# One matmul of 128 columns per level in the heads of a recurrent layer, with the second token half stored in another order

## The chip, the cores and the metric

The kernel runs on one core of a Trainium2 chip. The metric is the device time of one execution in microseconds (us), as the median of several runs.

## The reference, cut to what matters

A decoder trunk of two layers for 256 tokens of 2048 features. Layer 0 mixes tokens by two recurrences side by side, layer 1 by attention; an MLP follows each. The change concerns the second group of layer 0, eight heads (`hgrn2`) with 128 keys and 128 values each, and at its edge the first group (`rg_lru`).

```python
q = jax.nn.silu(q_raw.astype(F32))
log_f = jnp.log(lower_bound + (1.0 - lower_bound) * jax.nn.sigmoid(fz))
k = (1.0 - lower_bound) * jax.nn.sigmoid(-fz)
...
b = jnp.cumsum(gc, axis=2)
o_inter = jnp.einsum('bhtk,bhkv->bhtv', qc * jnp.exp(b), state)
decay = jnp.exp(jnp.where(causal, b[:, :, :, None, :] - b[:, :, None, :, :], -jnp.inf))
scores = jnp.einsum('bhtk,bhsk,bhtsk->bhts', qc, kc, decay)
o_intra = jnp.einsum('bhts,bhsv->bhtv', scores, vc)
```

So every query token sees every earlier key token of its head, each of the 128 key features damped by the product of the forget gates between the two tokens. The first group is a convolution over four tokens, two gates from block-diagonal products, a linear recurrence along the tokens, and a product with a GeLU branch.

## The kernel before, in words

**Matmuls.** TensorE (PE) multiplies 128x128 stationary blocks with moving columns. The inputs of the large products are split in two parts, `hi` and `lo`, and three products replace one (hi·hi, lo·hi, hi·lo). Weights come from HBM as `raw` tiles of 128x2048 by DMAs that SyncE (SP) issues. ScalarE (ACT) casts each into `hi` (L117) in two halves of 1024 columns, and VectorE (DVE) subtracts to get `lo` (L118). All three tiles have 3 buffers. The product itself is in `mm` (L205). What carries `bufa,hi` or `bufa,lo` in the profile are projections of the normed input, 48 matmuls of 256 columns (all tokens) for 128 features.

**The recurrent stage** (up to about 320 us of the span) is a list of steps in the string `ORDER` (L1172): `h0` to `h7` are the heads (`hgrn`), `x0` to `x7` the inputs of the first group (`lru_in`), `g0` and `g1` its gates (`lru_gates`, four blocks each), `y0` to `y7` its outputs (`lru_out`), `v`, `k`, `p` and `f` values, gates and prepared forms. A scheduler merges the steps' instructions when the kernel is built, with priorities that the source gives; on the chip each engine runs its list in order. So the string moves instructions on every engine.

**A head** projects q and f (two projections), then treats pairs of tokens (`pd`, L470), and then doubles: at level c = 2, 4, ..., 64 the tokens stand in blocks of 2c, and the second c queries of each block meet the first c keys. The tile `qk` holds q and k, 128 features on the partitions, 256 tokens each. A level (L483 to L514) is two f32 matmuls, one per half of 128 tokens (L492): the half's keys are the stationary block, all 128 of them, and 64 of its queries are the moving columns. The result `pl` has rows for all 128 keys, of which those in the right block are wanted. For c up to 16 a masked copy on DVE (L495) puts them into `st`; at c = 32 ACT copies two pieces of 32x64 (L500), at c = 64 one of 64x128 (L502). Then DVE scales q and k in place by the gates of the block (L509), for the next level, and makes the products of twice the length (L511). At c = 128 one matmul of 128 columns (L487) does the first half's keys against the second half's queries. `st` times the values gives `po` (L516 to L518); ACT squares it (L522), DVE norms it, and PE transposes it (L530) into `bufb`.

**lru_in** scales the projected block into `xp` (L538 and L418 in the profile), ACT applies the first tap (L540), DVE the other three (L542), and the result is split into `bufb` (ACT cast L250, DVE L251). **lru_gates** (L547) makes eight products of six matmuls from pairs of those blocks, each evicted by an ACT sigmoid (L234); tanh, exp and sqrt on ACT, products (L560) and a scan (L569) on DVE follow. **lru_out** multiplies its branch with the scan's result (L580). Projections and gate products share three PSUM banks (`p`), a level's result has two buffers (`pl`).

Of the kernel before, what the change touches and what calls it, by code (L numbers as in the profile page):

```python
# [10 lines left out]
F32 = mybir.dt.float32  # L11
# [9 lines left out]
P = 128  # L21
# [21 lines left out]
def trunk_kernel(ctx, tc, begin, xtok, cols, tab, masks, pos, fin, w_in, w_gate, w_out, w_qkv, w_o, w1, w2, out):  # L43
# [383 lines left out]
    def halves(t, c, second):  # L427
        return t.rearrange("p (n two c) -> p n two c", two=2, c=c)[:, :, int(second), :]
# [19 lines left out]
    def hgrn(hd, vg, gg):  # L448
        u0 = 20 + (hd // 4) * 16 + (hd % 4) * 2
        oml = omlb[:, hd:hd + 1]  # L450
        qk = wk.tile([P, 2 * S], F32, name="qk", bufs=3)
        qp, kq = qk[:, :S], qk[:, S:]
        p = project(w_in, u0, bufx)
        z = normed(p, "hz", 4)
        lut(qp, z, AF.Sigmoid)
        q3 = wk.tile([P, P, 3], F32, name="q3", bufs=2)
        pairs_ = lambda t: t.rearrange("p (n two) -> p n two", two=2)
        V.scalar_tensor_tensor(q3[:, :, :2], pairs_(z), oml, pairs_(qp), op0=OP.mult, op1=OP.mult)
        p = project(w_in, u0 + 1, bufx)
        z = normed(p, "hz", 4)  # L460
        f = wk.tile([P, S], F32, name="f", bufs=3)
        lut(f, z, AF.Sigmoid)
        lut(kq, z, AF.Sigmoid, scale=-1.0)
        V.tensor_scalar(f, f, oml, lb[:, hd:hd + 1], op0=OP.mult, op1=OP.add)
        f2 = pairs_(f)
        V.tensor_tensor(q3[:, :, 2], q3[:, :, 1], f2[:, :, 1], OP.mult)
        pd = psc.tile([P, P, 3], F32, name="pd", bufs=1)
        for j in range(2):
            js = slice(64 * j, 64 * j + 64)
            T.matmul(pd[:, js].rearrange("p n c -> p (n c)"), kq[:, j * P:j * P + P],  # L470
                     q3[:, js].rearrange("p n c -> p (n c)"), start=True, stop=True)
        st = wk.tile([P, 3, P], F32, name="st", bufs=3)
        V.tensor_tensor(st[:, :2].rearrange("p j (n two) -> p j n two", two=2),
                        pd[:, :, :2].rearrange("p (j n) c -> p j n c", j=2),
                        pairs_(ident)[:, None].to_broadcast([P, 2, 64, 2]), OP.mult)
        stf = st[:, :2].rearrange("p a b -> p (a b)")
        V.copy_predicated(halves(stf, 1, True), msk[:, 0].rearrange("p (n c) -> p n c", c=1), pd[:, :, 2:])
        V.tensor_tensor(pairs_(qp), q3[:, :, ::2], f2[:, :, :1].to_broadcast([P, P, 2]), OP.mult)
        V.tensor_tensor(pairs_(kq)[:, :, 0], pairs_(kq)[:, :, 0], f2[:, :, 1], OP.mult)
        tot = wk.tile([P, P], F32, name="tot128", bufs=2)  # L480
        V.tensor_tensor(tot, f2[:, :, 0], f2[:, :, 1], OP.mult)
        c = 2
        while c <= 128:  # L483
            pl = psc.tile([P, 2, 64], F32, name="pl", bufs=2)
            if c == 128:
                plf = pl.rearrange("p j c -> p (j c)")
                T.matmul(plf, kq[:, :P], qp[:, P:], start=True, stop=True)  # L487
                A.copy(st[:, 2], plf)
                break
            for j in range(2):  # L490
                js = slice(j * P, j * P + P)
                T.matmul(pl[:, j], kq[:, js], halves(qp[:, js], c, True), start=True, stop=True)  # L492
            if c <= 16:
                lv = LEVELS.index(c)
                V.copy_predicated(halves(stf, c, True), msk[:, lv].rearrange("p (n c) -> p n c", c=c),  # L495
                                  pl.rearrange("p j (n c) -> p (j n) c", c=c))
            elif c == 32:
                for n in range(2):
                    ps_ = slice(64 * n, 64 * n + 32)
                    A.copy(st[ps_, :2, 64 * n + 32:64 * n + 64], pl[ps_, :, 32 * n:32 * n + 32])  # L500
# [8 lines left out]
            V.tensor_tensor(both, both, fac, OP.mult)  # L509
# [6 lines left out]
        T.matmul(po[:, 0], st[:, 0], vg[:, 0, vs], start=True, stop=True)  # L516
        T.matmul(po[:, 1], st[:, 2], vg[:, 0, vs], start=True, stop=False)
# [15 lines left out]
    xc = wk.tile([P, 8, S], F32, name="xc", bufs=1)  # L533

    def lru_in(b):
        p = project(w_in, b, bufx)
        xp = wk.tile([P, S + 4], F32, name="xp", bufs=1)
        V.memset(xp[:, :4], 0.0)  # L538
        scaled(p, xp[:, 4:])
        A.activation(xc[:, b], xp[:, 4:], AF.Identity, bias=col("conv_b", b), scale=col("conv_w", 24 + b))  # L540
        for i in range(3):
            V.scalar_tensor_tensor(xc[:, b], xp[:, 1 + i:1 + i + S], col("conv_w", 8 * i + b), xc[:, b],  # L542
                                   op0=OP.mult, op1=OP.add)
        split_to(bufb[:, b], xc[:, b])
# [38 lines left out]
    def part_forms(f, k, m, at, src):  # L583
# [577 lines left out]
NOSYNC = mybir.DependencyInfo(mybir.DependencyClass.NoSync, mybir.DependencyReason.DATA)  # L1161


def _tables():
    ident = np.eye(P, dtype=np.float32)
    q = np.arange(S)[:, None]
    k = np.arange(S)[None, :]
    d = q - k
# [12 lines left out]
    for lv, c_ in enumerate(LEVELS):  # L1181
        col = np.arange(64)[None, :]
        m = (s // (2 * c_) == col // c_) & (s % (2 * c_) < c_)
        masks[:, lv, :64] = m
        masks[:, lv, 64:] = m
    return tab, masks


# [3 lines left out]
def _layout(a):  # L1192
# [33 lines left out]
    for what in ATTENTION:  # L1226
# [7 lines left out]
    xf = n(a["x"]).reshape(S, KB, P).transpose(2, 1, 0)  # L1234
    return {
        "begin": c(np.concatenate([xf, fv[:4].reshape(4, P, 4, 512).transpose(1, 0, 2, 3).reshape(P, KB, 512)], axis=2)),
        "xtok": c(n(a["x"]).reshape(2, P, D).transpose(1, 0, 2)),
        "cols": c(np.concatenate(cols, axis=1)),
        "tab": tab, "masks": masks,
        "pos": c(n(a["positions"]).reshape(2, P).T),  # L1240
        "fin": c(n(a["final_norm"]).reshape(1, D)),
        "w_in": c(np.concatenate(w_in)), "w_gate": c(w_gate), "w_out": c(toks(n(a["rec_w_out"][0]), [(k + 8) % KB for k in PAIRED])),
        "w_qkv": c(np.concatenate(w_qkv)), "w_o": c(toks(n(a["attn_w_o"][0]), PAIRED)),
# [20 lines left out]
```

## Time and profile before

| | |
|---|---|
| runs | 2122.53 us median of 3 (2121.95 to 2122.95) |
| profiled execution | 2123.78 us |
| its span | 2122.0 us |
| granted TensorE clock, mean | 0.999 |
| PE busy | 2111.1 us, 99% |
| DVE busy | 1807.3 us, 85% |
| ACT busy | 1383.3 us, 65% |

The profile is one execution. PE, DVE and ACT are the engines; PEld is the loading of stationary blocks, which can run beside PE's matmuls. A row of a timeline gives start, duration, engine, line of the source, operation, output and inputs, the stationary block's shape, and the moving shape. An f32 matmul leaves two records (x2), since it takes two passes. A list of waits gives for an engine's line whom it waited for, the total, how often, and the longest. A row of a group gives count, busy time, mean ns of one, and the idle time ahead of it.

### The profile page before, as it was taken

What the parts mean: (1) busy time and instruction counts of PE and PEld (TensorE: products, weight loads), DVE (VectorE), ACT (ScalarE), POOL (GpSimd) and SP (SyncE); (2) the same over time, 40 slices, a digit from 0 to 9 for tenths busy, and PEclk for the clock granted to TensorE, in tenths of its full rate; (3) what the DMA queues carried; (4) which work ended last, traced back from release to release, by engine and by line L of the source; (5) the groups of instructions that cost most, each with busy time, mean ns of one, the idle gap of its engine ahead of it and who ended that gap; (6) DMA issues with size and microseconds to landing.
All of it is one profiled execution on the core that took longest, in us unless ns stands there. A gap on an engine that the chain in (4) does not pass through costs nothing.

```text
span 2122.0 us, 26673 instructions
## 1 busy us (share of the span) xinstructions
PE 2111.1 (99%) x10492; PEld 1788.3 (84%) x10492; DVE 1807.3 (85%) x1998; ACT 1383.3 (65%) x1543; POOL 69.6 (3%) x89
## 2 busy tenths in 40 slices
PE   9999999999999999999999999999999999999998
PEld 8989998888888888888888888888888888888886
DVE  6987888888888888888987797798888887988887
ACT  7554666676576476567767777776755765755764
POOL 0000000000000000000000000000000000000000
PEclk9999999999999999999999999999999999999999
DMA  8565446877786777687887677777777768777874
GB/s 341 180 217 179 159 155 204 253 261 221 220 272 231 229 237 252 228 253 240 261 261 239 213 211 258 258 232 233 237 240 256 240 214 261 244 231 229 271 227 146
DMA packets 70382, 492.90 MB, mean 232 GB/s; under 512 B 7872, under 2 KB 8384, under 8 KB 12016
## 3 DMA queue, kind: packets, MB, share of 16 engines
q1 hardware_dynamic: 57888, 410.17, 51.6%
q0 software_dynamic: 11792, 79.89, 19.7%
q8 instruction: 82, 1.34, 0.2%
q10 hardware_dynamic: 576, 1.13, 0.1%
q14 instruction: 44, 0.36, 0.0%
HBM read 486.97 MB, written 4.19 MB: 231 GB/s over the span
## 4 chain that ended last, share of the span: by engine, by line
PE 98%; ACT 1%; DVE 1%; issue 0%; DMA 0%; SPq 0%; ACTq 0%; DVEq 0%
PE p L205 61%; PE po L205 14%; PE pd L205 13%; PE pt L205 5%; PE pl L208 2%; PE pl L492 1%; PE pl L205 0%; ACT hi L117 0%; ACT gi L234 0%; PE pd L208 0%; PE pd L470 0%; ACT L234 0%; DMA first<-in_begin 0%; ACT gr L234 0%; DVE xc L569 0%
## 5 line engine op out<-in xcount | busy, mean ns | idle before, releaser
L118 DVE TENSOR_TENSOR lo<-raw,hi 128x2048 fp32r<-128x2048 f32 (+2 forms) x388 | 784.8, 2028 | 152.5 <-ACT hi L117 148.3
L117 ACT CAST hi<-raw 128x2048 fp32r<-128x2048 f32 (+2 forms) x388 | 654.6, 1701 | 309.2 <-PE p L205 161.3
L205 PE MATMUL p<-hi,bufa 128*128 128x512 f32 x1448 | 470.5, 395 | 0.7 <-ACT hi L117 0.7
L205 PE MATMUL p<-hi,bufb 128*128 128x512 f32 x1160 | 373.9, 391 | 0.0
L205 PEld LDWEIGHTS p<-hi,bufa 128*128 128x128 f32 x1448 | 272.9, 189 | 57.0 <-ACT hi L117 1.0
L118 DVE TENSOR_TENSOR lo<-s,hi 128x2048 fp32r<-128x2048 f32 (+1 forms) x164 | 286.0, 1754 | 28.5 <-ACT hi L117 27.4
L117 ACT CAST hi<-s 128x2048 fp32r<-128x2048 f32 (+1 forms) x164 | 242.6, 1480 | 98.2 <-DVE s L173 54.1
L205 PE MATMUL p<-lo,bufa 128*128 128x512 f32 x724 | 280.7, 391 | 0.0
L205 PEld LDWEIGHTS p<-hi,bufb 128*128 128x128 f32 x1160 | 217.8, 188 | 44.9
L205 PE MATMUL p<-lo,bufb 128*128 128x512 f32 x580 | 225.8, 389 | 0.0
L205 PE MATMUL p<-bufa,hi 128*128 128x256 f32 x1024 | 188.0, 283 | 0.0
L205 PEld LDWEIGHTS p<-lo,bufa 128*128 128x128 f32 x724 | 136.5, 188 | 26.8
L205 PEld LDWEIGHTS p<-bufa,hi 128*128 128x128 f32 x1024 | 158.4, 189 | 0.2
L205 PE MATMUL p<-bufa,lo 128*128 128x256 f32 x512 | 145.1, 283 | 0.0
L117 ACT CAST hi<-t 128x2048 fp32r<-128x2048 f32 x41 | 78.5, 1914 | 99.5 <-PE p L205 91.0
L118 DVE TENSOR_TENSOR lo<-t,hi 128x2048 fp32r<-128x2048 f32 x41 | 94.0, 2292 | 56.0 <-ACT hi L117 55.8
L205 PEld LDWEIGHTS p<-lo,bufb 128*128 128x128 f32 x580 | 109.0, 188 | 22.0
L205 PE MATMUL p<-hi,formh 128*128 128x512 f32 x368 | 120.7, 391 | 0.0
L205 PE MATMUL p<-hi,formx 128*128 128x512 f32 x352 | 116.0, 391 | 0.0
L205 PE MATMUL po<-hi,bufb 128*128 128x512 f32 x320 | 103.8, 390 | 0.0
L205 PEld LDWEIGHTS p<-bufa,lo 128*128 128x128 f32 x512 | 96.7, 189 | 0.0
L173 DVE TENSOR_TENSOR s<-s,raw 128x1024 f32<-128x1024 f32 x82 | 96.4, 1218 | 0.1
(341 smaller groups left out, 3324.7 us busy)
## 6 DMA issues: line engine op xcount, KB each, us to landing
raw<-in_w SPq DMA_DIRECT2D x224, 1024.0 KB, 5.8
raw<-in_w_in SPq DMA_DIRECT2D x43, 1024.0 KB, 4.9
raw<-in_w_qkv SPq DMA_DIRECT2D x42, 1024.0 KB, 7.3
t<-in_w SPq DMA_DIRECT2D x32, 1024.0 KB, 5.1
t<-in_w POOLq DMA_DIRECT2D x32, 1024.0 KB, 9.0
s<-in_w POOLq DMA_DIRECT2D x17, 1024.0 KB, 8.7
raw<-in_w_out SPq DMA_DIRECT2D x15, 1024.0 KB, 5.0
raw<-in_w_o SPq DMA_DIRECT2D x14, 1024.0 KB, 8.1
```

The lines of the kernel that those rows point to most:

```text
L117: a = A.copy(h, w)
L118: v = V.tensor_tensor(l, w, h.bitcast(F32), OP.subtract)
L173: V.tensor_tensor(s, s, held["c"][:, at:at + 1024], OP.add)
L205: chain[:] = [after(T.matmul(*args, **kw), chain)]
L208: chain[:] = [after(T.transpose(out_, in_, ident), chain)]
L492: T.matmul(pl[:, j], kq[:, js], halves(qp[:, js], c, True), start=True, stop=True)
```

## The change

**Storage order.** The tokens of the second half are stored in another order (`PLACES`): position 128 + i holds token 128 + (i ^ 126), so the 64 pairs of tokens are reversed and the two tokens of a pair keep theirs. The host permutes x, positions, masks, tables and the output rows.

**Levels.** In `qk` the key halves change places, so that one regular pattern of 128 columns covers the level's queries of both halves. For c < 64 an ACT copy (L498) builds a block `mk` of 128 keys: of each half the 64 keys that the level needs. At c = 64 these are adjacent in `qk`. One f32 matmul of 128 columns (L501) takes the place of the two of 64. `mk` has two buffers. The masked copy is L505 now, the scaling L521; at c = 32 ACT copies four pieces of 32x32, at c = 64 two of 64x64 (L514). The level c = 128 is L493 and has the same shape as before. `hz` has three buffers instead of four.

**First group.** In `lru_in` the eviction is two operations of 128 columns (L557, and L558 with the pairs reversed), since the convolution needs the tokens in order; in `lru_out` the product with the scan's result is two (L599, L600).

**Order.** `ORDER` is another string. Among its differences: y2 stood between x7 and g1 and stands now ahead of x7; x5 stays behind g0, but x4 has moved from before g0 to before h6.

```diff
-        qp, kq = qk[:, :S], qk[:, S:]
+        at_ = lambda o, *dims: bass.AP(tensor=qk.tensor, offset=qk.offset + o, ap=[list(qk.ap[0])] + [list(d) for d in dims])
+        qp, kq = at_(0, (S + P, 2), (1, P)), at_(S, (-P, 2), (1, P))
+        k_of = lambda j: qk[:, S - j * P:S - j * P + P]
...
-        z = normed(p, "hz", 4)
+        z = normed(p, "hz", 3)
...
-            for j in range(2):
-                js = slice(j * P, j * P + P)
-                T.matmul(pl[:, j], kq[:, js], halves(qp[:, js], c, True), start=True, stop=True)
+            if c < 64:
+                mk = wk.tile([P, P], F32, name="mk", bufs=2)
+                A.copy(mk.rearrange("p (n e c) -> p n e c", e=2, c=c), at_(S, (2 * c, 64 // c), (c - P, 2), (1, c)))
+            else:
+                mk = qk[:, S - 64:S + 64]
+            T.matmul(pl.rearrange("p j c -> p (j c)"), mk,
+                     at_(c, (S + P - c, 2), (2 * c, 64 // c), (1, c)), start=True, stop=True)
             if c <= 16:
                 lv = LEVELS.index(c)
-                V.copy_predicated(halves(stf, c, True), msk[:, lv].rearrange("p (n c) -> p n c", c=c),
-                                  pl.rearrange("p j (n c) -> p (j n) c", c=c))
-            elif c == 32:
-                for n in range(2):
-                    ps_ = slice(64 * n, 64 * n + 32)
-                    A.copy(st[ps_, :2, 64 * n + 32:64 * n + 64], pl[ps_, :, 32 * n:32 * n + 32])
+                V.copy_predicated(bass.AP(tensor=st.tensor, offset=st.offset + c,
+                                          ap=[list(st.ap[0]), [P - c, 2], [2 * c, 64 // c], [1, c]]),
+                                  msk[:, lv].rearrange("p (j n c) -> p j n c", j=2, c=c),
+                                  pl.rearrange("p j (n c) -> p j n c", c=c))
             else:
-                A.copy(st[:64, :2, 64:], pl[:64])
+                for n in range(64 // c):
+                    for j in range(2):
+                        ks, qs = 2 * c * n + c * j, 2 * c * n + c * (1 - j)
+                        ps = (ks + 64) % P if c == 64 else ks
+                        A.copy(st[ks:ks + c, j, qs:qs + c], pl[ps:ps + c, j, c * n:c * n + c])
...
-        scaled(p, xp[:, 4:])
+        with urgent():
+            V.tensor_tensor(xp[:, 4:4 + P], p[:, :P], rs[:, :P], OP.mult)
+            V.tensor_tensor(flipped(xp, 4 + P), twos(p[:, P:S]), twos(rs[:, P:]), OP.mult)
...
-        V.tensor_tensor(y, y, xc[:, b], OP.mult)
+        V.tensor_tensor(y[:, :P], y[:, :P], xc[:, b, :P], OP.mult)
+        V.tensor_tensor(twos(y[:, P:]), twos(y[:, P:]), flipped(xc, b * S + P), OP.mult)
...
-ORDER = "v0 k0 f0 f1 f2 h0 h1 h2 x3 f3 x2 h3 x0 p1 x1 h4 h5 h6 x4 g0 x5 x6 y0 h7 y1 x7 y2 g1 y7 y4 y3 y6 y5"
+ORDER = "v0 k0 f0 f2 f1 h0 h1 x3 f3 h2 x2 h3 p1 x1 h4 h5 x0 x4 h6 g0 x5 x6 y1 h7 y0 y2 x7 g1 y7 y4 y3 y6 y5"
...
+PLACES = np.concatenate([np.arange(P), P + (np.arange(P) ^ (P - 2))])
```

What this moves on the engines, at the places of which the prediction speaks. PE before, where g1's products begin: `p_3323` is y2's projection, `p_3392` and `p_3400` are gate products, `qk_2970` is head h7.

```order
L205 MATMUL p_3323<-bufa_80,hi_3184 128x256 x2
L205 MATMUL p_3323<-bufa_80,lo_3185 128x256
L205 MATMUL p_3392<-bufb_189,hi_3251 128x256 x2
L205 MATMUL p_3392<-bufb_189,lo_3252 128x256
L492 MATMUL pl_3121<-qk_2970 128x64 x2
L205 MATMUL p_3392<-bufb_189,hi_3251 128x256 x2
L205 MATMUL p_3392<-bufb_189,lo_3252 128x256
L205 MATMUL p_3400<-bufb_189,hi_3251 128x256 x2
```

PE after, inside g1: `p_3483` and `p_3491` are its fourth and fifth product (the fifth's second part needs x7's block), `qk_3027` is head h7, `po_2690` is head h6's output.

```order
L205 MATMUL p_3483<-bufb_189,lo_3317 128x256
L205 MATMUL p_3491<-bufb_189,hi_3316 128x256 x2
L205 MATMUL p_3491<-bufb_189,lo_3317 128x256
L528 MATMUL po_2690<-vg_1592,st_2630 128x128
L501 MATMUL pl_3164<-qk_3027,mk_3165 128x128
L529 MATMUL po_2690<-vg_1592,st_2630 128x128
L530 MATMUL po_2690<-vg_1592,st_2630 128x128
L501 MATMUL pl_3172<-qk_3027,mk_3173 128x128
L205 MATMUL p_3491<-bufb_189,hi_3316 128x256
L501 MATMUL pl_3180<-qk_3027,mk_3181 128x128
L205 MATMUL p_3491<-bufb_189,hi_3316 128x256
```

Before, y2's 48 matmuls and more lay between x7's projection and the gates, and h7's levels stood two products and more apart. Now x7's projection (`p_3390`) ends right ahead of g1's first product, and three levels of h7 stand within the fifth.

DVE before, from the eviction of x7's projection (`p_3257`) to its split (L251 from `xc`):

```order
L418 TENSOR_TENSOR xp_3306<-p_3257,nr_237 128x256
L495 COPY_PREDICATED st_3100<-msk_200,pl_3107 128x64x2
L509 TENSOR_TENSOR qk_2970<-qk_2970,tot128_3105 128x2x64x2
L118 TENSOR_TENSOR lo_3318<-raw_3315,hi_3317 128x1024 x2
L542 SCALAR_TENSOR_TENSOR xc_290<-xp_3306,c__82,xc_290 128x256
L495 COPY_PREDICATED st_3100<-msk_200,pl_3114 128x32x4
L509 TENSOR_TENSOR qk_2970<-qk_2970,tot64_3112 128x2x32x4
L542 SCALAR_TENSOR_TENSOR xc_290<-xp_3306,c__82,xc_290 128x256 x2
```

DVE after, from the eviction of x7's projection to its last tap; `gi_3458` are the gates:

```order
L557 TENSOR_TENSOR xp_3439<-p_3390,nr_237 128x128
L558 TENSOR_TENSOR xp_3439<-p_3390,nr_237 128x64x2
L118 TENSOR_TENSOR lo_3452<-raw_3449,hi_3451 128x1024
L521 TENSOR_TENSOR qk_2500<-qk_2500,tot4_2678 128x2x2x64
L118 TENSOR_TENSOR lo_3452<-raw_3449,hi_3451 128x1024
L251 TENSOR_TENSOR bufb_189<-z_3371,bufb_189 128x256
L561 SCALAR_TENSOR_TENSOR xc_290<-xp_3439,c__82,xc_290 128x256
L579 TENSOR_TENSOR xc_290<-xc_290,gi_3458 128x256
L561 SCALAR_TENSOR_TENSOR xc_290<-xp_3439,c__82,xc_290 128x256
L579 TENSOR_TENSOR xc_290<-xc_290,gi_3458 128x256
L505 COPY_PREDICATED st_3157<-msk_200,pl_3164 128x2x32x2
L521 TENSOR_TENSOR qk_3027<-qk_3027,tot128_3162 128x2x64x2
```

The eviction is in two parts, and the gates' own products (L579, which was L560) now stand among the taps (L561, which was L542). On ACT, the copies `mk` of h7 stand between evictions and the cast of x7's block:

```order
L234 ACTIVATE gi_3458<-p_3483,c__82 128x256
L534 ACTIVATE ho_2694,hs_2695<-po_2690 128x128 x2
L498 COPY mk_3173<-qk_3027 128x128
L250 CAST bufb_189<-xc_290 128x256
L498 COPY mk_3181<-qk_3027 128x128
L234 ACTIVATE gr_3457<-p_3491,c__82 128x256
L498 COPY mk_3189<-qk_3027 128x128
```

No such copy was there before. At g0 the gates' first product `p_2729` stands right behind h6's f projection `p_2571`, on DVE this way (`qk_1928` is h4):

```order
L521 TENSOR_TENSOR qk_1928<-qk_1928,tot8_2095 128x2x4x32
L418 TENSOR_TENSOR hz_2620<-p_2571,nr_237 128x256
L118 TENSOR_TENSOR lo_2722<-raw_2719,hi_2721 128x1024
L521 TENSOR_TENSOR qk_1928<-qk_1928,tot4_2106 128x2x2x64
L118 TENSOR_TENSOR lo_2722<-raw_2719,hi_2721 128x1024
```

Before, x4's projection stood between them, and h4's last scaling stood further behind, after a head's preparation (L464 to L481) and its products.

More of the change, by code (lines that the diff above doesn't have):

```diff
@@ L469, in hgrn @@
             js = slice(64 * j, 64 * j + 64)
-            T.matmul(pd[:, js].rearrange("p n c -> p (n c)"), kq[:, j * P:j * P + P],
+            T.matmul(pd[:, js].rearrange("p n c -> p (n c)"), k_of(j),
                      q3[:, js].rearrange("p n c -> p (n c)"), start=True, stop=True)
@@ L477, in hgrn @@
         V.copy_predicated(halves(stf, 1, True), msk[:, 0].rearrange("p (n c) -> p n c", c=1), pd[:, :, 2:])
-        V.tensor_tensor(pairs_(qp), q3[:, :, ::2], f2[:, :, :1].to_broadcast([P, P, 2]), OP.mult)
-        V.tensor_tensor(pairs_(kq)[:, :, 0], pairs_(kq)[:, :, 0], f2[:, :, 1], OP.mult)
+        V.tensor_tensor(qpp, both_of(q3)[:, :, :, ::2], both_of(f2[:, :, :1].to_broadcast([P, P, 2])), OP.mult)
+        k_even = at_(S, (-P, 2), (2, 64))
+        V.tensor_tensor(k_even, k_even, by_half(f2[:, :, 1]), OP.mult)
         tot = wk.tile([P, P], F32, name="tot128", bufs=2)
@@ L533, in trunk_kernel, with flipped @@
     xc = wk.tile([P, 8, S], F32, name="xc", bufs=1)
+    twos = lambda t: t.rearrange("p (n two) -> p n two", two=2)
+    def flipped(t, o):
+        return bass.AP(tensor=t.tensor, offset=t.offset + o + P - 2, ap=[list(t.ap[0]), [-2, 64], [1, 2]])
     def lru_in(b):
@@ L1167, in _tables @@
     k = np.arange(S)[None, :]
-    d = q - k
+    d = PLACES[q] - PLACES[k]
     c = ((d >= 0) & (d <= 128)).astype(np.int32) + ((d >= 0) & (d % 4 == 0)) + ((d >= 0) & (d % 16 == 0))
@@ L1184, in _tables @@
         masks[:, lv, :64] = m
-        masks[:, lv, 64:] = m
+        masks[:, lv, 64:] = m if c_ == 1 else (s // (2 * c_) == col // c_) & (s % (2 * c_) >= c_)
     return tab, masks
@@ L1233, in _layout @@
     c = np.ascontiguousarray
-    xf = n(a["x"]).reshape(S, KB, P).transpose(2, 1, 0)
+    x = n(a["x"]).reshape(S, D)[PLACES]
+    xf = x.reshape(S, KB, P).transpose(2, 1, 0)
     return {
         "begin": c(np.concatenate([xf, fv[:4].reshape(4, P, 4, 512).transpose(1, 0, 2, 3).reshape(P, KB, 512)], axis=2)),
-        "xtok": c(n(a["x"]).reshape(2, P, D).transpose(1, 0, 2)),
+        "xtok": c(x.reshape(2, P, D).transpose(1, 0, 2)),
         "cols": c(np.concatenate(cols, axis=1)),
         "tab": tab, "masks": masks,
-        "pos": c(n(a["positions"]).reshape(2, P).T),
+        "pos": c(n(a["positions"]).reshape(S)[PLACES].reshape(2, P).T),
         "fin": c(n(a["final_norm"]).reshape(1, D)),
@@ L1262 @@
     o = r.results[0]["out_0"]
[L1263 removed]
+    return np.ascontiguousarray(o.transpose(1, 0, 2).reshape(S, D)[PLACES].reshape(1, S, D))
```

14 lines of the change are left out of this document (8 added, 6 removed).

## The prediction

> **What bounds the kernel now.** I read the busy times and the chain that ended last first.
>
> ```profile
> span 2122.0 us, 26673 instructions
> ...
> PE 2111.1 (99%) x10492; PEld 1788.3 (84%) x10492; DVE 1807.3 (85%) x1998; ACT 1383.3 (65%) x1543; POOL 69.6 (3%) x89
> ...
> PE 98%; ACT 1%; DVE 1%; issue 0%; DMA 0%; SPq 0%; ACTq 0%; DVEq 0%
> ```
>
> TensorE (PE) is busy for 99% of the span and makes 98% of the chain: time taken off PE shortens the kernel as long as PE still waits for nobody. What PE waits for today, in the whole span:
>
> ```profile
> PE po L264 <- DVE xp L538: 1.1, 1, 1.1
> PE p L205 <- ACT hi L117: 0.7, 1, 0.7
> PE pl L492 <- DVE qk L509: 0.3, 1, 0.3
> PE po L517 <- ACT st L488: 0.2, 1, 0.2
> ```
>
> Only the last two (0.5 us together) concern the heads. So the cover is complete now, and the question is how thin it is. The windows show it (us from the start, then PE, PEld, DVE, ACT busy in 20 us):
>
> ```profile
> 200.00:220.00 20.00, 20.00 (x172) 20.00 (x171) 17.09 (x52) 8.32 (x14) 0.00 (x0) 1.00 0.45 158
> 220.00:240.00 20.00, 20.00 (x172) 20.00 (x171) 16.40 (x55) 17.23 (x35) 0.00 (x0) 1.00 0.45 154
> 240.00:260.00 20.00, 19.71 (x172) 19.51 (x171) 19.97 (x48) 13.27 (x26) 0.00 (x0) 1.00 0.46 159
> 300.00:320.00 20.00, 19.80 (x170) 19.60 (x169) 19.96 (x48) 14.37 (x28) 0.00 (x0) 1.00 0.47 159
> ```
>
> In most of the stage VectorE (DVE) has 15 to 20% of its time left and ScalarE (ACT) more. Around the two gate blocks, at 240 to 260 and 300 to 320, DVE has nothing left (19.97 and 19.96 of 20). That is where PE waits today, and where I expect the new waits. The granted clock is 1.00 throughout.
>
> **The change, part by part: what PE saves.** A level of today is two matmuls of 64 columns. One stands here, inside a stream of 256-column matmuls:
>
> ```profile
> 84.36 0.39 PE L205 MATMUL p<-bufa,hi 128*128 128x256 f32 x2
> ...
> 84.70 0.39 PE L205 MATMUL p<-bufa,hi 128*128 128x256 f32 x2
> 84.92 0.55 PE L492 MATMUL pl<-qk 128*128 128x64 f32 x4
> 85.28 0.36 PE L205 MATMUL p<-bufa,lo 128*128 128x256 f32 x1
> 85.49 0.40 PE L205 MATMUL p<-bufa,hi 128*128 128x256 f32 x2
> ```
>
> Each f32 matmul is two records, so x4 is one level. Starts count, since matmuls overlap. Undisturbed, three of the stream take 84.70 − 84.36 = 0.34 us. With a level among them they take 85.49 − 84.70 = 0.79: **a level costs 0.45 us**. A 128-column f32 matmul with a 128x128 stationary block, the form that the change uses, stands here:
>
> ```profile
> 101.08 0.28 PE L205 MATMUL p<-bufa,hi 128*128 128x256 f32 x1
> 101.20 0.38 PE L516 MATMUL po<-vg,st 128*128 128x128 f32 x2
> ...
> 101.54 0.28 PE L205 MATMUL p<-bufa,lo 128*128 128x256 f32 x1
> ```
>
> From 101.08 to 101.54 is 0.46, less two stream matmuls (2 × 0.115): **0.23 us**. So a level saves 0.22. There are 6 such levels in each of 8 heads, as the count of the first row says (192 records, 4 a level); the second row is the level of c = 128, which is unchanged:
>
> ```profile
> L492 PE MATMUL pl<-qk 128*128 128x64 f32 x192 | 26.6, 261 | 0.3 <-DVE qk L509 0.3
> L487 PE MATMUL pl<-qk 128*128 128x128 f32 x16 | 3.1, 272 | 0.0
> ```
>
> 48 × 0.22 = **−10.6 us** on PE (0.21 to 0.23 a level by the reading: −10.1 to −11.0). The Trainium skill, "TensorE: Matmul & The Clock Gate", section "Back-to-back issue gap", speaks against this: its gap grows with the moving columns, about 60 cycles up to 64 columns and 134 for 128, so two narrow matmuls would cost no more than a wide one, and the sum on PE would be nothing. Its section "LDWEIGHTS (loading the stationary operand)" has a load go by the block's columns, 128/1.2 = 107 ns; by that two loads fewer in a level would be an estimated 0.21 us, 10.2 us in all. The trace agrees with the second: 0.45 against 0.23 for the same columns.
>
> **What is added on ACT.** For c = 2 to 32 the stationary block `mk` is an ACT copy, 5 × 8 = 40. No row is this copy. Below is the 128x128 copy of L488 at 0.254 us, above it the 128x256 cast of L250 at 0.403; I take 0.25, the nearer in size, so 40 × 0.25 = 10 us. Copies of results go from 3 to 6 a head (c = 32: four, c = 64: two): 24 more at about L500's 0.2, 5 us.
>
> ```profile
> L117 ACT CAST hi<-raw 128x1024 fp32r<-128x1024 f32 x74 | 73.9, 1047 | 45.9 <-issue 28.6 <-PE p L205 14.7 <-ACT st L500 1.6
> L234 ACT ACT_TABLE_LOAD x7 | 9.0, 1283 | 0.1
> L250 ACT CAST bufb<-xc 128x256 fp32r<-128x256 f32 x8 | 3.2, 403 | 1.1 <-DVE xc L542 1.1
> L500 ACT COPY st<-pl 32x64 f32<-32x64 f32 x16 | 3.2, 199 | 3.4 <-PE pl L492 3.3
> L488 ACT COPY st<-pl 128x128 f32<-128x128 f32 x8 | 2.0, 254 | 2.0 <-PE pl L487 2.0
> ```
>
> The 15 us of throughput lie beside PE: ACT is busy 8 to 17 of 20 us above. The latency matters more: `mk` is a new step between the scaling on DVE (L509) and the level's matmul. How much room is there? Once in a projection, and once at the gates:
>
> ```profile
> 106.06 0.46 DVE L509 TENSOR_TENSOR qk<-qk,tot 128x256 f32<-128x256 f32 x1
> 109.10 0.55 PE L492 MATMUL pl<-qk 128*128 128x64 f32 x4
> ...
> 247.21 0.40 DVE L509 TENSOR_TENSOR qk<-qk,tot 128x256 f32<-128x256 f32 x1
> 247.53 1.22 DVE L118 TENSOR_TENSOR lo<-raw,hi 128x1024 fp32r<-128x1024 f32 x1
> 247.66 0.66 PE L492 MATMUL pl<-qk 128*128 128x64 f32 x4 [0.29 <-DVE qk L509]
> ```
>
> In the projection 109.10 − 106.52 = 2.58 us are left. A copy with two hops of 0.05 (as 247.61 to 247.66) needs 0.35, and 2.4 if a whole pair of hi casts (2 × 1.047) stands ahead of it: covered, with little over. At the gates nothing is left: PE waited 0.29.
>
> **What is added on DVE.** The evictions of 8 lru_in steps and the products of 8 lru_out steps are cut in two: 16 × (2 × 0.283 − 0.42) = 2.3 us, by L479's 128x128 and L418's 128x256.
>
> ```profile
> L118 DVE TENSOR_TENSOR lo<-raw,hi 128x1024 fp32r<-128x1024 f32 x76 | 91.9, 1220 | 11.6 <-ACT hi L117 11.1
> L509 DVE TENSOR_TENSOR qk<-qk,tot 128x256 f32<-128x256 f32 x48 | 20.4, 424 | 1.0 <-PE pl L492 0.9
> L542 DVE SCALAR_TENSOR_TENSOR xc<-xp,c__82,xc 128x256 f32<-128x256 f32 x24 | 11.5, 479 | 0.1
> L495 DVE COPY_PREDICATED st<-msk,pl 128x128 f32<-128x128 int8 x32 | 10.7, 334 | 1.3 <-PE pl L492 1.0
> L418 DVE TENSOR_TENSOR xp<-p,nr 128x256 f32<-128x256 f32 x8 | 3.4, 420 | 0.7 <-PE p L205 0.6
> L560 DVE TENSOR_TENSOR xc<-xc,gi 128x256 f32<-128x256 f32 x8 | 3.3, 422 | 0.0
> L479 DVE TENSOR_TENSOR qk<-qk,f 128x128 f32<-128x128 f32 x8 | 2.3, 283 | 0.0
> ```
>
> The other masks, reversed pairs and strides keep counts and sizes; I cost them at 0 (an eighth on L495's 10.7 us would be 1.3, on an engine that has room outside the gates). Fewer buffers for `hz`, the tables and the host's order move no instruction that I can price: 0, with the room above as cover. DMA shares are 0.45 to 0.48, and SP's and POOL's rows stand as before.
>
> **What is moved: the order of steps.** The step string changes too. At **g1**, x7's projection now stands right before the gates that need its block; before, y2's projection stood between. The chain from x7's last matmul to the fifth gate product: drain 0.17 (0.28 recorded against 0.115 of spacing), hop 0.05; then on DVE two half evictions 0.56, lo half 1.22, a scaling 0.42, lo half 1.22, L251 0.42, three L542 and two L560 among them up to the last L542 (3 × 0.479 + 2 × 0.422), a masked copy 0.33, a scaling 0.42 = 6.9 us of durations. Back to back, DVE starts the next some 0.09 before a duration is over:
>
> ```profile
> 100.23 0.42 DVE L473 TENSOR_TENSOR st<-pd,tab__196 128x256 f32<-128x256 f32 x1
> 100.56 0.28 DVE L479 TENSOR_TENSOR qk<-qk,f 128x128 f32<-128x128 f32 x1
> ```
>
> Less 12 × 0.085 that is 5.9. With the cast of L250 (0.40) and two hops: 6.6 us. PE has until then four gate products of six matmuls (4 × 0.70), half a product (0.35) and seven small f32 matmuls (7 × 0.23): 4.75. Wait: **1.9**. Then only one stream matmul stands between h7's levels `pl_3172` and `pl_3180`, whose chain (masked copy, scaling, `mk`, hops) is some 0.9 longer than what ran meanwhile: **0.8**. PE works in order: behind the waiting product stand h7's levels and g1's other products, so nothing fills the wait. Sum for g1 2.7 (bounds 0, if DVE takes the scalings late, and 4.5, if each lo half also waits a cast).
>
> At **g0** the gates now stand right behind h6's f projection. For h4's c = 128 the drain, hop, scaling and hop take 0.17 + 0.05 + 0.42 + 0.05 = 0.69 against a product of 0.70, if DVE is free; but a lo half stands ahead (0 to 1.22, I take 0.6), and an `mk` of h5 stands behind ACT table loads (0 to 1.28, I take 0.3): **0.9**. Last head's po, behind two ACT copies where one was and behind a table load: **0.5** (0 to 1.3). All other `mk` copies: two of forty late by one copy, **0.5** (0 to 4, a tenth of a microsecond each).
>
> **The sum**, against the profiled execution's 2123.78 us (its span of 2122.0 and 1.8 around it): −10.6 on PE, −0.5 for the two waits of today, which lie at places that are reordered, + 2.7 + 0.9 + 0.5 + 0.5 of new waits = −6.5, so 2117.3. The profiled execution lies 1.25 above the median of the runs, 2122.53, so I forecast **2116.0**.
>
> **Rivals.**
> - *No new wait at all*: the new order hides them. −10.6 − 0.5 − 1.25 gives 2111.4. For it: 2.58 us of room at an ordinary level. Against it: g1's count above.
> - *DVE becomes the bound in the last four heads.* DVE has 19.97 and 19.96 of 20 around the gates, and 2.3 us are added. What PE saves there (half of 10.6) is then waited away, on top of the 2.7 of g1: −10.6 − 0.5 + 5.3 + 2.7 = −3.1, about 2119.5. Against it: 16.4 and 17.09 of 20 in the windows between.
> - *Slower: the `mk` copy gates every level.* ACT works in order, and a copy behind a pair of hi casts needs 2.4 us of the 2.58. If the levels stand closer to their scalings than today, each copy makes PE wait. From a mean of 0.27 us over 40 copies the gain is gone (10.6/40); from 0.37 the kernel is slower by more than 4.2 us. At 0.5 it is + 20 − 11.1 = + 8.9: 2131.4. For it: L117 is ACT's largest group, 73.9 us. Against it: most copies meet an ACT that is idle a third of the time.
> - *The change doesn't do what it says*: PE's time goes by columns, which stay. Then nothing is saved and the waits stay: −0.5 + 4.6, 2126.6. Against it: the two windows at 84 and 101. The issue-gap rule of the Trainium skill's page "TensorE: Matmul & The Clock Gate" (section "Back-to-back issue gap") would come out here.
>
> **How the numbers follow.** 0.2%, about what a measurement of this kernel can tell from no change, is 4.2 us: faster is below 2118.3. The forecast (2113.5 to 2118.5) has 0.47, no new wait 0.12, the DVE bound 0.23, the copies 0.13, no saving 0.05. Faster: 0.47 + 0.12 less 0.01 of its edge = 0.58; the same: the DVE bound, the edge and no saving = 0.29; slower 0.13. The range leaves out the two last (0.18): low 2111 by full saving, high 2123 by the DVE bound with g0 at its upper end (+ 1.9) and copies late by another 1.5.
>
> **What would show it.** L501 must have 96 records, and a level among stream matmuls 0.23 us; 0.45 would make the saving wrong. PE's waits must show p behind L250's cast and pl behind `mk` at g1, 2 to 4 us together, a microsecond at g0, and hardly any elsewhere. If waits behind `mk` are spread over the heads, the copies decide; if they stand behind L521 over whole windows with DVE at 20 of 20, DVE does; if g1 has none, I placed its chain wrong. ACT should gain about 15 us, DVE about 2. PE's busy time outside the stage must stay, else something other than this decides.

## The result, and the profile after

The changed kernel takes **2115.59 us** (median of 6 runs, 2114.17 to 2116.49) against 2122.61 us before (6 runs, 2121.58 to 2123.04): a ratio of 0.9967, 95% interval 0.9956 to 0.9978. That is 7.0 us less, and 0.4 us from the forecast of 2116.0.

The profiled execution took 2115.5 us. Its page, from the top:

```profile
span 2113.7 us, 26567 instructions
...
PE 2099.5 (99%) x10396; PEld 1775.9 (84%) x10396; DVE 1809.1 (86%) x2014; ACT 1397.6 (66%) x1607; POOL 69.6 (3%) x89
```

PE has 96 records fewer and 11.6 us less busy time, ACT 14.3 us more, DVE 1.8 more. The two profiled executions are 8.3 us apart, and 1.3 of this lies ahead of the changed code: the first projection starts at 50.74 us in the changed kernel and at 52.09 before. In the execution before, the granted clock rose to 1.00 at 9.86 us, in the changed kernel's at 4.07, and PE's first large matmuls ran at half pace for longer (the first four took 7.88 − 6.01 = 1.87 us there, and 6.95 − 5.92 = 1.03 in the changed kernel). Before:

```profile
6.01 2.07 PE L205 MATMUL p<-hi,bufa 128*128 128x512 f32 x4 [0.75 <-ACT hi L117]
7.88 1.05 PE L205 MATMUL p<-lo,bufa 128*128 128x512 f32 x2
```

After:

```profile
5.92 1.19 PE L205 MATMUL p<-hi,bufa 128*128 128x512 f32 x4 [1.17 <-ACT hi L117]
6.95 0.62 PE L205 MATMUL p<-lo,bufa 128*128 128x512 f32 x2
```

The other 6.9 us arise in the recurrent stage. From its end to the end of the kernel, the two executions keep the same distance to within 0.05 us.

A level inside a stream of 256-column matmuls, from the timeline of PE (start, duration, line, operation, count of records):

```profile
74.55 0.39 PE L205 MATMUL p<-bufa,hi 128*128 128x256 f32 x2
74.77 0.39 PE L501 MATMUL pl<-qk,mk 128*128 128x128 f32 x2
74.91 0.37 PE L205 MATMUL p<-bufa,lo 128*128 128x256 f32 x1
75.12 0.40 PE L205 MATMUL p<-bufa,hi 128*128 128x256 f32 x2
```

From 74.55 to 75.12 is 0.57 us; three stream matmuls of 0.115 in it leave 0.225 for the level. Before it was 0.45.

What PE waits for, in the whole span (line waited at, releaser, total, times, longest):

```profile
PE pl L501 <- ACT mk L498: 1.8, 2, 1.1
PE p L205 <- ACT hi L117: 1.4, 2, 1.2
...
PE pl L493 <- DVE qk L521: 0.8, 2, 0.4
PE po L528 <- ACT st L514: 0.4, 1, 0.4
```

Of forty copies `mk`, only two keep PE waiting, both in g1. The two waits for `hi` lie in the first 10 us of the kernel, ahead of the changed code (in the other runs of this study they sum to 0.5 to 1.6 us). The timeline of PE in g1:

```profile
271.37 0.46 PE L493 MATMUL pl<-qk 128*128 128x128 f32 x2 [0.36 <-DVE qk L521]
...
273.33 0.40 PE L501 MATMUL pl<-qk,mk 128*128 128x128 f32 x2
...
275.25 0.49 PE L501 MATMUL pl<-qk,mk 128*128 128x128 f32 x2 [1.08 <-ACT mk L498]
275.69 0.38 PE L205 MATMUL p<-bufb,hi 128*128 128x256 f32 x1
276.79 0.49 PE L501 MATMUL pl<-qk,mk 128*128 128x128 f32 x2 [0.71 <-ACT mk L498]
...
278.79 0.63 PE L205 MATMUL p<-bufb,hi 128*128 128x256 f32 x2
279.22 0.41 PE L205 MATMUL p<-bufb,lo 128*128 128x256 f32 x1
279.43 0.63 PE L205 MATMUL p<-bufb,hi 128*128 128x256 f32 x2
```

The reader sees two things. The waits stand at h7's second and third level (pl behind mk), so x7's block, which I expected to be late first, was in time by then. And behind the waits the stream runs at half its pace: three matmuls take 279.43 − 278.79 = 0.64 us instead of 0.345. The granted clock says why (windows cut where the clock changes; the first number behind the comma is PE's busy time, the column behind the bracketed count of POOL is the clock):

```profile
273.73:277.14 3.41, 1.62 (x10) 1.09 (x10) 3.18 (x15) 1.65 (x8) 0.00 (x0) 1.00 0.72 286
277.14:280.55 3.41, 3.41 (x19) 3.41 (x18) 2.32 (x11) 1.38 (x4) 0.00 (x0) 0.50 0.00 0
280.55:283.97 3.42, 3.42 (x31) 3.42 (x31) 2.42 (x4) 3.12 (x6) 0.00 (x0) 1.00 0.02 5
```

Sixteen matmuls at 0.213 us instead of 0.115 lose 1.6 us, nearly as much as the two waits themselves. PE counts as fully busy in the second window, so this loss is in no list of waits.

The list leaves out something else too. At g0 PE waits 0.43 us for h4's last scaling:

```profile
213.52 0.28 PE L205 MATMUL p<-bufb,lo 128*128 128x256 f32 x1
214.22 0.46 PE L493 MATMUL pl<-qk 128*128 128x128 f32 x2 [0.43 <-DVE qk L521]
214.61 0.51 PE L205 MATMUL p<-bufb,hi 128*128 128x256 f32 x2
```

From the stream matmul ahead of this level to the one behind it are 1.09 us. Without a wait it is 0.25 (the median over 30 levels in the stream). So this wait costs 0.84 us, twice what the list says: in the stream the records overlap (0.28 us recorded, the next start after 0.115), and around the wait they hardly do.

Why was `mk` late? DVE in g1:

```profile
269.67 1.22 DVE L118 TENSOR_TENSOR lo<-raw,hi 128x1024 fp32r<-128x1024 f32 x1 [0.48 <-ACT hi L117]
270.81 0.42 DVE L521 TENSOR_TENSOR qk<-qk,tot 128x256 f32<-128x256 f32 x1
...
273.35 0.48 DVE L561 SCALAR_TENSOR_TENSOR xc<-xp,c__82,xc 128x256 f32<-128x256 f32 x1
273.78 0.42 DVE L579 TENSOR_TENSOR xc<-xc,gi 128x256 f32<-128x256 f32 x1
274.13 0.43 DVE L505 COPY_PREDICATED st<-msk,pl 128x128 f32<-128x128 int8 x1
274.36 0.46 DVE L521 TENSOR_TENSOR qk<-qk,tot 128x256 f32<-128x256 f32 x1
274.73 0.48 DVE L561 SCALAR_TENSOR_TENSOR xc<-xp,c__82,xc 128x256 f32<-128x256 f32 x1
```

DVE works without a gap from 269.67. h7's first level started on PE at 273.33 and took 0.40, but its scaling (the last row but one) starts at 274.36, behind a tap, a gate product and the masked copy. Then `mk` takes 0.30 on ACT, and PE goes on at 275.25. The last row is x7's last tap, which comes after the scaling.

### The profile page after: what moved, and what is told of

It reads as the page before. It is cut to its first block, busy times and chain, and to the rows that moved or that the text cites. A ratio compares the mean times of both kernels' runs of the same rounds, so it can differ in the third digit from the quotient of the medians.

```text
span 2113.7 us, 26567 instructions
## 1 busy us (share of the span) xinstructions
PE 2099.5 (99%) x10396; PEld 1775.9 (84%) x10396; DVE 1809.1 (86%) x2014; ACT 1397.6 (66%) x1607; POOL 69.6 (3%) x89
## 4 chain that ended last, share of the span: by engine, by line
PE 98%; ACT 1%; DMA 0%; DVE 0%; issue 0%; SPq 0%; ACTq 0%; DVEq 0%
PE p L205 62%; PE po L205 14%; PE pd L205 13%; PE pt L205 5%; PE pl L208 2%; PE pl L205 0%; PE pl L501 0%; ACT hi L117 0%; DMA first<-in_begin 0%; PE pd L208 0%; PE pd L475 0%; ACT gi L234 0%; ACT L234 0%; PE po L528 0%; PE po L529 0%
```

## The experiments

Each is the changed kernel with one edit, where nothing else is said. The scheduler rebuilds all lists for every one of them. "Room" is the time from the last level of h7 (c = 128) to the last projection matmul of the stage: what PE still has to do while h7's norm and transposes are under way. "End waits" are PE's waits behind the last projection.

| run | median us | ratio to before (95%) | room | end waits |
|---|---|---|---|---|
| before | 2122.5 to 2122.9 | 1 | 23.1 | 0 |
| changed | 2115.59 | 0.9967 (0.9956 to 0.9978) | 16.0 | 0 |
| e1 old string | 2120.54 | 0.9992 (0.9982 to 1.0001) | −2.6 | 6.8 |
| e2 new string, old levels | 2125.53 | 1.0015 (1.0006 to 1.0025) | 33.4 | 0 |
| e3 y2 between | 2117.82 | 0.9978 (0.9968 to 0.9988) | 4.5 | 4.2 |
| e4 two of 64 | 2132.93 | 1.0049 (1.0034 to 1.0064) | 5.0 | 4.1 |
| e5 urgent levels | 2115.46 | 0.9966 (0.9953 to 0.9978) | 23.1 | 0 |
| e6 no mk | 2115.48 | 0.9967 (0.9954 to 0.9980) | 27.1 | 0 |
| e7 mk twice | 2133.38 | 1.0049 (1.0034 to 1.0064) | −19.3 | 11.1 |
| e8 changed, again | 2116.33 (one run) | | | |
| e9 split later, urgent | 2119.92 | 0.9986 (0.9977 to 0.9995) | 10.1 | 3.5 |
| e10 split later | 2118.95 | 0.9983 (0.9974 to 0.9992) | 4.5 | 3.7 |

**e1, the new levels in the old string.**

```diff
-ORDER = "v0 k0 f0 f2 f1 h0 h1 x3 f3 h2 x2 h3 p1 x1 h4 h5 x0 x4 h6 g0 x5 x6 y1 h7 y0 y2 x7 g1 y7 y4 y3 y6 y5"
+ORDER = "v0 k0 f0 f1 f2 h0 h1 h2 x3 f3 x2 h3 x0 p1 x1 h4 h5 h6 x4 g0 x5 x6 y0 h7 y1 x7 y2 g1 y7 y4 y3 y6 y5"
```

> The changed levels with the step string of before. My theory: PE saves 0.23 us in each of 48 levels whatever the order (11.0), and the waits of g1 (pl behind mk, 1.8 us) and the halved clock behind them (about 1.5 us) belong to the new string, since y2's 48 matmuls stand between x7 and g1 again; the 0.29 us at g0 of before comes back with up to 1 us of mk: 2112.5 to 2114.5, PE waiting behind mk less than 1 us in all. Rival, the new string is what hides the copies: in the old string the levels wait behind mk for more than 3 us and the time is 2116 or more.

Measured: 2120.54 us. My expectation fell. The rival has the time but not the cause: the waits behind `mk` are small, as I said (0.4 us in all), but a wait that neither of the two had makes up for it. PE at the end of the stage:

```profile
306.21 0.28 PE L205 MATMUL p<-bufa,lo 128*128 128x256 f32 x1
...
308.82 0.39 PE L493 MATMUL pl<-qk 128*128 128x128 f32 x2
...
320.94 0.66 PE L542 MATMUL pt<-tab__196,ho 128*128 128x128 f32 x2 [6.28 <-DVE ho L539]
322.17 0.80 PE L205 MATMUL p<-hi,bufb 128*128 128x512 f32 x1 [0.56 <-ACT bufb L253]
```

The last projection's last matmul starts at 306.21, and h7's last level comes after it. `po`, the norm and the transposes then have only a part of the output projection beside them, and PE waits 6.28 us, with the clock at 0.50 behind it, from 318.87 to 325.70. Before the change the same two points stand the other way round, 23 us apart:

```profile
296.99 0.38 PE L487 MATMUL pl<-qk 128*128 128x128 f32 x2
...
320.04 0.28 PE L205 MATMUL p<-bufa,lo 128*128 128x256 f32 x1
```

So the heads' levels, which follow one another head by head, end 11.8 us later in the same string (308.82 against 296.99). That is 0.30 us for each of the 40 levels that got an `mk`, and a copy takes 0.299 us; but the match is not shown to be more than chance. In the new string the new levels end only 5.9 us later than the old ones do (295.56 against 289.64, e2).

**e2, the old levels in the new string** (the kernel before with only `ORDER` changed).

> The levels of before (two matmuls of 64 columns, no mk) with the new step string. My theory: x7 right ahead of g1 makes a wait there from DVE's queue even without mk, 1.5 to 2.5 us, and perhaps 1.5 us of halved clock: 2124 to 2127. Rival, the waits of g1 come from mk alone: no wait over 0.5 us there, 2121.5 to 2123.

Measured: 2125.53 us, as expected. Without `mk` PE still waits in g1 (the first row, and one of the second row's two waits; the other lies at 243 us):

```profile
PE pl L492 <- DVE qk L509: 0.9, 1, 0.9
PE po L516 <- ACT st L502: 0.7, 2, 0.3
```

Behind these waits the clock is at 0.50 from 289.86 to 293.28. So the new string by itself costs 3 us, and DVE's queue makes the longest wait. But it brings h7's last level 7 us forward (289.64), and its room to 33 us, which the old levels had no use for.

**e3, y2 back between x7 and g1.**

```diff
-... y1 h7 y0 y2 x7 g1 y7 ...
+... y1 h7 y0 x7 y2 g1 y7 ...
```

> The changed kernel with y2 back between x7 and g1, nothing else. My theory: the 1.8 us of waits behind mk in g1 go and with them the 3.5 us at half clock (15 matmuls at 0.213 instead of 0.115 us, 1.5 us): 2112 to 2113.5, granted clock 1.00 in every 20 us of the stage. Rival, the wait only moves (to the levels of h7 behind another DVE queue): 2115 to 2116.5, with waits of 1.5 us or more elsewhere in the stage.

Measured: 2117.82 us, 2.2 slower than the changed kernel. The waits of g1 behind `mk` went, as I said, but they moved: the rival was right about that, though the time is 1.3 us above its range too. PE's waits, the two largest, and h7's last level and the last projection:

```profile
PE pt L542 <- DVE ho L539: 2.2, 1, 2.2
PE p L205 <- DVE bufb L254: 1.4, 1, 1.4
```

```profile
303.67 0.38 PE L493 MATMUL pl<-qk 128*128 128x128 f32 x2
...
308.12 0.28 PE L205 MATMUL p<-bufa,lo 128*128 128x256 f32 x1
```

The room is 4.5 us here and 16 in the changed kernel. There, PE's list puts three levels of h7 within 4 us (273.33, 275.25, 276.79), and PE waits for two of them; here the same three stand 3 and 6 us apart (275.14, 278.22, 284.35) and need no wait. So the closeness that makes the wait in g1 also buys room at the end.

**e4, two matmuls of 64 columns on the same block.**

```diff
-            T.matmul(pl.rearrange("p j c -> p (j c)"), mk,
-                     at_(c, (S + P - c, 2), (2 * c, 64 // c), (1, c)), start=True, stop=True)
+            for j in range(2):
+                T.matmul(pl[:, j], mk, at_(c + j * (S + P - c), (2 * c, 64 // c), (1, c)), start=True, stop=True)
```

> The changed kernel, but each level again as two matmuls of 64 columns on the same block mk; all copies and masks stay. My theory: a level costs 0.45 us instead of 0.23, so 48 levels add 10 to 11 us to PE: 2124.5 to 2127.5. Rival, PE goes by moving columns and the gain came from elsewhere (order, fewer waits): 2115 to 2117.

Measured: 2132.93 us, 17.3 above the changed kernel and 5 above the upper end that I expected. A level alone answers as expected:

```profile
85.36 0.28 PE L205 MATMUL p<-bufa,hi 128*128 128x256 f32 x1
85.47 0.55 PE L502 MATMUL pl<-qk,mk 128*128 128x64 f32 x4
85.83 0.36 PE L205 MATMUL p<-bufa,hi 128*128 128x256 f32 x1
86.03 0.28 PE L205 MATMUL p<-bufa,lo 128*128 128x256 f32 x1
```

0.67 less two stream matmuls is 0.44 us, so PE goes by the number of matmuls here and not by columns: 48 × 0.215 = 10.3. Each of these matmuls loads its block again (192 loads beside 192 matmul records), so this run doesn't tell the load from the matmul. Of the other 7 us, 3.0 are further waits in the stage (room 5.0, 4.1 us of end waits), 1.0 more time lost at half clock, 0.9 a slower spacing of the stream (787 matmuls at 0.113 us, 977 in the changed kernel) and 0.7 lie ahead of the changed code; the last 1.4 I can't place one by one.

**e5, scalings and copies with priority.**

```diff
-                A.copy(mk.rearrange("p (n e c) -> p n e c", e=2, c=c), at_(S, (2 * c, 64 // c), (c - P, 2), (1, c)))
+                with urgent():
+                    A.copy(mk.rearrange("p (n e c) -> p n e c", e=2, c=c), at_(S, (2 * c, 64 // c), (c - P, 2), (1, c)))
...
-            V.tensor_tensor(both, both, fac, OP.mult)
+            with urgent():
+                V.tensor_tensor(both, both, fac, OP.mult)
```

> The changed kernel, with the scaling of a level (DVE) and the copy mk (ACT) given the priority that evictions have, so that they stand earlier in their engines' queues. My theory: the waits of g1 come from the scaling's place in DVE's queue (behind two gate products and two taps), and the levels of the eight heads form one chain, whose end lies close to the stage's end in the changed kernel; an earlier scaling shortens both: waits of g1 from 1.8 to at most 1.3 us, no wait of pt behind ho, 2112.5 to 2115.5. Rival: what the levels overtake (lo halves, casts) comes late instead, and PE waits for weights or evictions by more than 2 us: 2116 to 2120.

Measured: 2115.46 us, within what I expected, and no different from the changed kernel. h7's last level comes 7.5 us earlier (288.02), and g1's waits shrink a little, but some 16 matmuls at half clock stand behind them again (1.6 us):

```profile
PE pl L502 <- ACT mk L499: 1.1, 2, 0.9
```

**e6, no copies** (the levels below 64 take the block of c = 64).

```diff
-            if c < 64:
-                mk = wk.tile([P, P], F32, name="mk", bufs=2)
-                A.copy(mk.rearrange("p (n e c) -> p n e c", e=2, c=c), at_(S, (2 * c, 64 // c), (c - P, 2), (1, c)))
-            else:
-                mk = qk[:, S - 64:S + 64]
+            mk = qk[:, S - 64:S + 64]
```

> The changed kernel without the 40 copies: all levels take the adjacent block of c = 64 as stationary block, so levels below 64 multiply the wrong keys. My theory: 11 us of ACT time and 0.3 us of each level's chain go; ACT's time alone is worth nothing, but the waits behind mk in g1 (1.8 us) shrink to 1.2 or less with the next scaling as the releaser: 2112.5 to 2115. Rival, the copies cost throughout: 2108 or less, by waits that vanish all over the stage (there are only 3.3 us of new ones).

Measured: 2115.48 us, 0.5 above the upper end that I expected, and no different from the changed kernel. The 12 us that the copies take on ACT are worth nothing to this string, though h7's last level comes 10.5 us earlier without them (285.05). The wait in g1 did not shrink, and the clock was at 0.50 behind it again, for 3.4 us. PE goes on at 276.85; the list names a small step of a head's norm (L312, over at 276.78), right behind the level's scaling (over at 276.70), which I had expected:

```profile
PE pl L497 <- DVE rs L312: 1.7, 1, 1.7
```

**e7, each copy twice.** The line with `A.copy(mk...)` stands twice.

> The changed kernel with each of the 40 copies mk done twice, so 11.4 us more on ACT and 0.3 us more in each level's chain. My theory, the chain of levels bounds the stage's end: h7's levels fall behind all projections, and PE waits there for the head's norm (pt behind ho, as with the old string), 4 us or more, with the clock halved behind it: 2121 to 2132. Rival, the copies lie beside PE's work: at most 1 us more than the changed kernel, 2115 to 2117.

Measured: 2133.38 us, a little above the upper end. PE waits at the end of the stage, as I expected, and behind the norm (pt) by what I expected; the waits behind `mk`, all but 0.3 us of them at the end too, I had not expected:

```profile
PE pl L502 <- ACT mk L499: 5.5, 3, 3.9
PE pt L543 <- DVE ho L540: 5.0, 2, 3.6
```

h7's last level stands at 329.62, 34 us later than in the changed kernel: 0.85 us for each copy, though a second copy takes 0.3. About 7 us of the 34 are longer waits ahead of that level, and some 4 are lost at half clock behind them; the rest is still about twice the copies' 12 us. So the levels' pace is not the chip's alone. It is written into PE's list when the kernel is built, and in the changed kernel this list leaves 2 us and more between the end of an `mk` and its matmul at 32 of the 40 levels (median 2.3).

**e8, the changed kernel once more.**

> The changed kernel once more, as it is. Waits of g1 and the half clock behind them should be there again at the same places if they belong to the program (1.1 and 0.7 us, then 3 to 4 us at half clock), and the share of 256-column matmuls at 0.113 us spacing (977 of 1498 in its first profile, 506 of 1482 before the change) should be the same if that does too; if it is chance, the share lies elsewhere.

Measured: waits of 1.07 and 0.71 us at the same two levels, then 16 matmuls at half clock again: these belong to the program. The faster spacing does so only in part: 864 of 1498 stream matmuls were at 0.113 us this time, 977 of 1498 in the first profile. The two executions differ in two stretches (51 to 69 and 281 to 288 us in the first) and agree nearly everywhere else.

**e9 and e10, a split of weights behind x7's taps.** The two casts and two lo halves that stand ahead of x7's taps are ordered behind them (in e9 with the priority of e5).

```diff
+            for i, one in ((a, hold[:1]), (v, hold[1:])):
+                after(i, one)
...
+        taps[b] = [first.ins.name, last.ins.name]
...
+        hold[:] = taps[7] if gp else []
         w = unit(w_gate, gp)
+        hold[:] = []
```

> The changed kernel with two edits: the split of one weight tile (two casts on ACT, two lo halves on DVE, 2.4 us) is ordered behind x7's taps instead of ahead of them, and scalings and mk have the priority of evictions as in e5. My theory: g1's waits are the time that x7's taps and h7's first scaling lose behind that split, so they go (under 0.4 us left there), with no half clock behind them, and the earlier scalings let h7 end in time: 1.8 + 1.6 us less than the changed kernel, 2111.5 to 2113. Rival: h7's levels, no longer pushed together by the wait, end late, and PE waits at the stage's end behind ho as in the run with y2 between: 2115.5 to 2119.

> As the one before, without the priority of scalings and mk. My theory: g1's waits go here too, but h7's last level comes some 100 matmuls later than in the changed kernel, where the run with y2 between had it, so PE waits at the stage's end (pt behind ho and bufb, 3 to 5 us, then some microseconds at half clock): 2116.5 to 2119. Rival: the wait at the stage's end was of y2's place, not of the levels' pace: 2111.5 to 2114.

Measured: e10 2118.95 us and e9 2119.92 us. In e10 the waits behind `mk` are gone from g1, room is 4.5 us and PE waits 3.7 us at the end: as expected. e9 failed in both respects. In g1 other waits came (for an eviction and for x7's block, which stood behind the same lo halves again), and the room of 10.1 us was too little:

```profile
PE p L207 <- DVE bufb L256: 2.0, 1, 2.0
PE p L207 <- ACT bufb L255: 1.6, 1, 1.6
PE p L207 <- DVE bufb L253: 1.2, 1, 1.2
```

No version beat the changed kernel.

## Why the prediction was right, point by point

**The saving on PE** was forecast as 48 × 0.22 = 10.6 us. The profile has 0.45 − 0.225 a level, 10.8. That one matmul in place of two saves this much, and not that columns decide, is what e4's level (0.44 us for the same columns on the same block) shows: the row that I put against the Trainium skill's issue-gap table holds, and the rival "no saving" is out. I read that section, "Back-to-back issue gap", too narrowly: it gives the table for a matmul by itself, and says ahead of it that in a stream of loads and matmuls both set the spacing, which is what the rows show.

**The waits** were forecast as 4.6 us in new places, less 0.5 for the two old ones. By PE's list they are smaller: g1 2.2 against 2.7 forecast (0.36 + 1.08 + 0.71), g0 0.43 against 0.9, po of the last head 0.41 against 0.5, the other copies nothing against 0.5; 3.0 in all. But the forecast counted delays from start to start. Counted so, with the overlap that a wait takes away, g1 costs 3.5 (6.3 us from 270.73 to 277.03, where its 18 matmuls would take 2.8 in the stream), g0 0.84 and po 0.68: 5.0 in all; and the two old waits, which went, cost 1.0 and not 0.5. So the forecast was about right in the sum, but too small in g1, and the other copies cost nothing. Within g1 the step "to the fifth gate product" failed as it stood: I expected 1.9 us at the product and 0.8 at the level behind it, and PE waited 1.08 and 0.71 at the two levels, and 0.36 at h6's last level, which I had not counted at all. The instructions that I added up are the right ones, but I had x7's last tap ahead of the level's scaling, and it stands behind it; so the level was the first that PE missed.

**What I left out** is the price of a lower clock behind a wait: 1.6 us behind g1. What hides it in the sum is a term that I had left out too: in the profiled executions 977 of 1498 stream matmuls are at 0.113 us and the others mostly at 0.118, before 506 of 1482, which saves about 2.1 us (1.6 by the second profile of the changed kernel). That these two nearly cancel is luck, and with it that the forecast is off by only 0.4 us. From the first projection to the stage's end the sum is −10.8 from the levels, + 5.0 − 1.0 of waits, + 1.6 of half clock and about −2.1 of spacing: −7.3, where the profiles have −6.9; the difference of 0.4 I can't place. The medians of the runs differ by 7.0.

**The rival that DVE becomes the bound** is out: in every 20 us from 180 to 320 us DVE was busy for 15.3 to 19.5, and PE waited behind L521 for 0.8 us in the whole kernel.

**The costs at nothing** held: ACT got 14.3 us more (15 forecast, an `mk` being 0.299 us and not 0.25), DVE 1.8 (2.3 forecast), both beside PE's work. e6 shows it for the copies in this string.

**The new string** I read wrongly, though the sum did not need it: I counted only what it costs. e1 and e2 show its other side. With the old levels it loses 3 us; with the new ones it gains 5, since in the old string the new levels end 11.8 us later, behind the last projection. The rival that "each `mk` gates its level" had the wrong mechanism (two of forty did), but the copies do add up, in the end of the chain (e6: 10.5 us earlier without them; e7: 34 us later with each done twice). e1, e3, e4, e7, e9 and e10 all have end waits, and all have a room of about 10 us or less; the runs with 16 us or more have none.

**Still open**: that the levels' pace comes from PE's list, which leaves 2 us between most copies and their matmuls, is argued from e7, not shown; a list with all levels closer wasn't tried. No run tells whether a level's saving is that of a load or of a matmul.

## What to carry to other kernels

Where PE bounds and a matmul has few columns, count the matmuls: two of 64 columns that became one of 128 saved 0.22 us here. What the merger adds to each step of a serial chain shows only at the chain's end: measure the time between the chain's last step and the end of the work that hides it, before and after, and not only the slack at each step. A wait that such a chain needs can be moved, and each time this study moved it away from one place, it came back at the other.

## What the runs showed of the hardware

**A short wait can cost twice.** In g1, 1.08 and 0.71 us of waits within 3 us were followed by a granted clock of 0.50 for 3.41 us. In e5 it was 0.93, 0.28 and 0.18 us, with the same slow matmuls behind them. Single waits of up to 1.02 us (e7, at 215 us) had no such price in any run. But the sum of the waits alone doesn't decide it: e9 had 0.83 and 1.23 us within 3 us, and the clock stayed. The traces show why. In each of the twelve profiles all changes of the clock lie whole multiples of 3.413 us apart (in the changed kernel it rises at 4.07 us, falls at 277.14, 80 times 3.413 later, and rises at 280.55). So the clock goes by stretches of that length, whose place differs from execution to execution. The waits of g1 fell into one stretch (273.73 to 277.14, with 1.79 us of idle PE; the rows are in the section on the result). Those of e9 fell into two, with 0.83 and 1.23 us:

```profile
273.47:276.88 3.41, 2.58 (x21) 2.27 (x20) 3.37 (x7) 3.41 (x8) 0.00 (x0) 1.00 0.00 0
276.88:280.29 3.41, 2.18 (x17) 1.86 (x16) 3.17 (x12) 1.72 (x8) 0.00 (x0) 1.00 0.47 125
```

In the first 600 us of all profiles, no stretch at full clock with less than 1.25 us of idle PE was followed by a fall, and each of the eleven with 1.6 us or more was; between, it went either way (in e2 the clock fell after 1.27 us, in e9 it stayed after 1.55). The Trainium skill, "TensorE: Matmul & The Clock Gate", Part 1 on the clock gate, has the clock fall to half after an idle window of about 3.4 us, with a window that runs free of the program. The depth, the length and the free run agree (0.50, 3.41 us, rises at 4.07 to 10.64 us in the twelve profiles). That it takes an idle window of that length does not: about half of one was enough here.

**The stream has two paces.** Matmuls of 256 columns with the same operands follow each other at 0.113 or at 0.118 us over stretches of many, and a small matmul among them can change one into the other (before the change, 0.34 us for three at 84.36, and 0.35 at 85.49, behind a level). The share of the fast pace differed between two executions of the same program (977 and 864 of 1498), which is 0.5 us and may be part of the spread of the runs.
